# Feed-forward of a two-layer decoder trunk: down's block differences made during gate/up on VectorE and kept in DRAM, roundings moved from GpSimd to ScalarE

## The chip, the cores and the metric

The kernel runs on one core of one Trainium2 chip. The metric is device time in microseconds (us) of one execution. Engines are named as the profile names them: PE (TensorE), DVE (VectorE), ACT (ScalarE), POOL (GpSimd), SP (SyncE, whose queue issues every DMA here).

## The reference

One sequence of 1024 tokens, width 1024, passes two residual layers (an attention mixer, then a feed-forward of hidden width 2816), and a last RMSNorm. Only the feed-forward is touched:

```python
def swiglu(h, w_gate, w_up, w_down):
    return (jax.nn.silu(h @ w_gate) * (h @ w_up)) @ w_down

for layer in range(DEPTH):                  # DEPTH = 2
    ...
    h = rmsnorm(x, norm_ffn[layer])
    x = x + swiglu(h, ffn_w_gate[layer], ffn_w_up[layer], ffn_w_down[layer])
return rmsnorm(x, norm_final)
```

## The kernel before

All products are float32. Each operand is split into a rounded part `hi` (type float32r) and the rest `lo = x - hi`, and `mm3` issues three matmuls for a pair (hi·hi, hi·lo, lo·hi). `round_to` makes `hi` (a copy on ACT or a `tensor_scalar` on POOL), and `rest_of` makes `lo` with one two-operand subtraction.

The feed-forward uses Strassen-like 2x2 block products: seven instead of eight, at the price of sums and differences of blocks. `ffn` has three stages for each layer (names begin with f0 or f1):

- `ffn_prep` finishes the output projection, normalizes, and makes the blocks b11, b21, b22 and the differences t1 to t4 of the activations, all kept in SBUF as hi and lo.
- `gate_up(p)`, for p from 0 to 10, takes 256 hidden columns. For gate (g) and for up (u) it loads two 512 KB tiles `raw` (tag "raw", three buffers for the whole kernel), splits a11, a12, a22, forms s1 to s4 from them (`f0g5u` and the like are the tiles of these sums) and splits those. `product` runs seven block products of 12 matmuls each, so a p has 168 matmuls of 512 columns. PSUM results are drained into tiles ea, e4, e7; silu and the multiplication by u follow, then s1, s2, s4, s3 of the activations (ec, ed). Seven activation blocks go to DRAM (`act_da`, `act_ds`).
- `down` runs seven left blocks m (the table `plan`) against right blocks of w_down, each over four row tiles t: 28 steps (m, t) of 33 matmuls, 924 in all. A step needs its activation tile (`load_act`: two loads `ar`, rounding on ACT, rest, names f0a0 to f0a27) and the right block's hi and lo (`weights(m)`: six pieces d0 to d2, loads `dr`, names f0d00 to f0d62). After each step the result in PSUM (tile o, two buffers) is added to one to four accumulators `c`.

Before, a right block with a sign in the plan is made inside `down` from the block before it: a fresh piece of w_down is loaded, and hi and lo of the previous piece are subtracted from it by two two-operand instructions, the first always on POOL, the second on POOL or DVE in turn:

```python
    ph, pl = (v.bitcast(F32) for v in before[u // 2][1])
    second = nc.vector if u % 4 else nc.gpsimd
    if sign < 0:
        nc.gpsimd.tensor_tensor(raw, raw, ph, op=ALU.subtract)
        second.tensor_tensor(raw, raw, pl, op=ALU.subtract)
```

Each engine runs its own instructions in the program's order, and so does SP with the DMAs. That order is written by a scheduler which ranks instructions by a simulated timeline; a buffer is given to a new tile when the old one's last reader is through.

Of the kernel before, what the change touches and what calls it, by code (L numbers as in the profile page):

```python
# [11 lines left out]
F32 = mybir.dt.float32  # L12
F32R = mybir.dt.float32r
# [26 lines left out]
def trunk(ctx: ExitStack, tc: tile.TileContext, x, norm_mix, norm_ffn, norm_final,  # L40
# [89 lines left out]
    def unit8(name, b, f, hl):  # L130
        return hp.tile([128, 4, 512], F32R, name=name, tag=f"h{b}{f}{hl}")
# [698 lines left out]
    def gate_up(layer, p, name, fp, h):  # L830
        def weights(src, nm):
            raw = []
            for b in range(2):
                r = wp.tile([128, 1024], F32, name=f"{nm}r{b}", tag="raw", bufs=3).rearrange("p (k n) -> p k n", n=256)
                nc.sync.dma_start(r, src[b * 512:(b + 1) * 512, p * 256:(p + 1) * 256].rearrange("(k p) n -> p k n", p=128))
                raw.append(r)
            a11, a21, a12, a22 = (raw[b][:, :, i * 128:(i + 1) * 128] for b in range(2) for i in range(2))
            w = {}
            hl = fp.tile([128, 2, 4, 128], F32R, name=f"{nm}a", tag="wa", bufs=2)
            hl = [hl[:, i] for i in range(2)]  # L840
            early = nc.vector if p == 0 else nc.gpsimd
            round_to(nc.gpsimd if p else nc.scalar, hl[0], a11)
            rest_of(nc.vector, hl[1], a11, hl[0])
            w["a11"] = [(hl[0][:, k, :], hl[1][:, k, :]) for k in range(4)]

            def two(keys, src, wpool, tag, hi_eng, bufs):
                hi, lo = (wpool.tile([128, 1024], F32R, name=f"{nm}{keys[0]}{x}", tag=tag + t, bufs=bufs)
                          .rearrange("p (k n) -> p k n", n=256) for x, t in (("h", "hi"), ("l", "lo")))
                round_to(hi_eng, hi, src)
                rest_of(nc.vector, lo, src, hi)  # L850
                for i, key in enumerate(keys):
                    cs = slice(i * 128, (i + 1) * 128)
                    w[key] = [(hi[:, k, cs], lo[:, k, cs]) for k in range(4)]

            two(("a12", "a22"), raw[1], wp, "w", nc.gpsimd, 3)
            u1, u2 = (fp.tile([128, 4, 256], F32, name=f"{nm}u{i}", tag="wu", bufs=2) for i in range(2))
            s2, s3, s1, s4 = u1[:, :, 0:128], u1[:, :, 128:256], u2[:, :, 0:128], u2[:, :, 128:256]
            early.tensor_tensor(s1, a21, a22, op=ALU.add)
            early.tensor_tensor(s2, s1, a11, op=ALU.subtract)
            early.tensor_tensor(s3, a11, a21, op=ALU.subtract)  # L860
            two(("s2", "s3"), u1, fp, "vw", nc.scalar, 3)
            early.tensor_tensor(s4, a12, s2, op=ALU.subtract)
            two(("s1", "s4"), u2, fp, "vw", nc.scalar, 3)
            return w

        def product(src, nm):

            w = weights(src, nm)
            a, c, b = ps_s(f"{nm}oa")[:, 0, :], ps_t(f"{nm}oc"), ps_t(f"{nm}ob")
            ea = fp.tile([128, 2, 512], F32, name=f"{nm}ea", tag="ea", bufs=3)  # L870
            e = {k: fp.tile([128, 512], F32, name=f"{nm}e{k}", tag=f"e{k}", bufs=n) for k, n in ((4, 3), (7, 1))}
            e[1], e[2] = ea[:, 0], ea[:, 1]

            def times(o, left, right, start):

                for k in range(4):
                    r = tuple(v[:, k, :] for v in h[right])
                    mm3(o, w[left][k], r, start and k == 0, k == 3, not start)

            times(a, "a11", "b11", True)  # L880
            nc.scalar.copy(e[1], a)
            times(c, "a12", "b21", True)
            nc.vector.tensor_tensor(e[1], c, e[1], op=ALU.add)
            times(a, "s2", "t2", False)
            nc.scalar.copy(e[2], a)
            times(b, "s3", "t3", True)
            nc.scalar.copy(e[7], b)
            times(a, "s1", "t1", False)
            nc.scalar.copy(e[4], a)
            nc.gpsimd.tensor_tensor(e[4], e[4], e[7], op=ALU.add)  # L890
            times(b, "a22", "t4", False)
            nc.vector.tensor_tensor(e[2], b, e[2], op=ALU.add)
            times(a, "s4", "b22", False)
            return [e[1], a, e[2], e[4]]

        g = product(ffn_w_gate[layer], f"{name}g{p}")
        u = product(ffn_w_up[layer], f"{name}u{p}")
        def store(key, v):
            q = p // 6
            nc.sync.dma_start(act_d[key, q][:, :, p - q * 6, :].rearrange("t p c -> p t c"),  # L900
                              v.rearrange("p (t c) -> p t c", c=128))
# [12 lines left out]
        add.tensor_tensor(s1, av["a21"], av["a22"], op=ALU.add)
        store("s1", s1)
        add.tensor_tensor(s2, s1, av["a11"], op=ALU.subtract)
        store("s2", s2)
        add.tensor_tensor(s4, av["a12"], s2, op=ALU.subtract)
        store("s4", s4)
        add.tensor_tensor(av["a21"], av["a11"], av["a21"], op=ALU.subtract)  # L920
        store("s3", av["a21"])

    def down(layer, name, fq, fp, last):

# [6 lines left out]
        plan = (("a11", 0, 0, 0, ((0, 0), (0, 1), (1, 0), (1, 1))),
                ("s1", 0, 1, -1, ((0, 1), (1, 1))),
                ("s2", 1, 1, -1, ((0, 1), (1, 0), (1, 1))),
                ("a22", 1, 0, -1, ((1, 0),)),
                ("a12", 1, 0, 0, ((0, 0),)),
                ("s4", 1, 1, 0, ((0, 1),)),
                ("s3", 0, 1, 1, ((1, 0), (1, 1))))

        w = {}

        def weights(m):
            _, bi, bj, sign, _ = plan[m]
            before = w.get(m - 1)
            w[m] = []
            for u in range(0, nk, 2):
                if u % 4 == 0:
                    i = u // 4
                    if m % 2:
                        hl = [unit8(f"{name}d{m}{i}{x}", (0, 0, 1)[i], (0, 1, 0)[i], x) for x in "hl"]
                    else:  # L950
                        hl = [fq.tile([128, 4, 512], F32R, name=f"{name}d{m}{i}{x}", tag=f"q{('b21', 't3', 't1')[i]}{x}")
                              for x in "hl"]
                n = min(2, nk - u)
                raw = wp.tile([128, 1024], F32, name=f"{name}dr{m}{u}", tag="raw", bufs=3)[:, :n * 512]
                raw = raw.rearrange("p (k n) -> p k n", n=512)
                nc.sync.dma_start(raw, w_down[bi][:, u:u + n, bj * 512:(bj + 1) * 512])
                if sign:
                    ph, pl = (v.bitcast(F32) for v in before[u // 2][1])
                    second = nc.vector if u % 4 else nc.gpsimd
                    if sign < 0:  # L960
                        nc.gpsimd.tensor_tensor(raw, raw, ph, op=ALU.subtract)
                        second.tensor_tensor(raw, raw, pl, op=ALU.subtract)
                    else:
                        nc.gpsimd.tensor_tensor(raw, ph, raw, op=ALU.subtract)
                        second.tensor_tensor(raw, raw, pl, op=ALU.add)
                hi, lo = (v[:, u % 4:u % 4 + n, :] for v in hl)
                round_to(nc.scalar if sign or u % 4 else nc.gpsimd, hi, raw)
                rest_of(nc.vector, lo, raw, hi)
                w[m].append((u, (hi, lo)))
                yield  # L970
# [5 lines left out]
        def load_act(s):  # L976
            m, t = divmod(s, 4)
            whole = s % 2 and m < 6
            if whole:
                both = [hp.tile([128, nk, 128], F32R, name=f"{name}a{s}{x}", tag=f"h11{x}") for x in "hl"]  # L980
            out_ = []
            for g, (k0, k1) in enumerate(GROUPS):
                raw = fp.tile([128, 1024], F32, name=f"{name}ar{s}{g}", tag="wu", bufs=2)[:, :(k1 - k0) * 128]
# [258 lines left out]
```

## Time and profile before

| | before |
|---|---|
| median of 3 runs | 2891.46 us (2885.41 to 2892.29) |
| profiled execution, its own time | 2894.9 us |
| span of the profile | 2893.1 us |
| PE busy, share of the span | 2689.0 us, 93% |
| DVE, ACT, POOL busy | 1835.9, 1183.9, 1246.5 us |
| mean granted TensorE clock | 0.969 |

The span is what the profile's times are counted in, from its start at 0. Layer 0's feed-forward lies between about 780 and 1518 us in it, layer 1's between about 2160 and the end.

### The profile page before, as it was taken

The numbers are of one execution on the slowest core, as the hardware profiler recorded it, in microseconds if no ns is written. First come the engines' busy times: TensorE is split into PE (matmuls) and PEld (weight loads), VectorE is DVE, ScalarE is ACT, GpSimd is POOL, SyncE is SP. The second block draws the span as 40 slices with busy tenths as digits, with TensorE's granted clock in tenths as the row PEclk, the third lists the DMA queues.
The fourth block names the chain that finished last, engine by engine and source line by source line (L and its number), as shares of the span: only waits on it lengthen the run. The fifth ranks groups of instructions, "written<-read, shape, count | busy, mean of one in ns | idle before, by whom it ended". The sixth has DMA issues, their size and how long they took to land.

```text
span 2893.1 us, 42415 instructions
## 1 busy us (share of the span) xinstructions
PE 2689.0 (93%) x15596; PEld 2324.1 (80%) x15596; DVE 1835.9 (63%) x2822; ACT 1183.9 (41%) x2545; POOL 1246.5 (43%) x1119
## 2 busy tenths in 40 slices
PE   8999999989889999987999899999888999998798
PEld 7989898988868888866778788787886888886676
DVE  7477677565484444379654867778848444447965
ACT  4277666454252222222333555555415222222233
POOL 3566554543156656446352021212015656554623
PEclk9999999999989999999999999999998999999999
DMA  5100000113523333454553333324452333345454
GB/s 152 45 9 22 9 21 21 52 44 104 175 83 109 106 109 103 136 187 150 181 172 78 71 79 69 92 71 105 131 179 88 110 106 109 97 141 186 148 183 138
DMA packets 285855, 301.54 MB, mean 104 GB/s; under 512 B 22448, under 2 KB 233040, under 8 KB 285648
## 3 DMA queue, kind: packets, MB, share of 16 engines
q1 hardware_dynamic: 285648, 298.83, 34.5%
q8 instruction: 124, 2.03, 0.3%
q14 instruction: 83, 0.68, 0.1%
HBM read 200.72 MB, written 72.88 MB: 95 GB/s over the span
## 4 chain that ended last, share of the span: by engine, by line
PE 62%; DVE 15%; issue 8%; DMA 7%; ACT 4%; POOL 3%; SPq 0%; POOLq 0%; DVEq 0%; ACTq 0%
PE sqo L126 2%; PE sqo L127 2%; PE sqo L128 2%; DMA f0dr<-in_ffn_w_down_dram 1%; PE svo L126 1%; PE svo L127 1%; PE svo L128 1%; DMA f1ar<-act_da 1%; PE oao L126 1%; PE oao L127 1%; PE oao L128 1%; DVE f0c L1015 1%; DVE f1c L1015 1%; DMA f1dr<-in_ffn_w_down_dram 1%; DMA f0ar<-act_da 1%
## 5 line engine op out<-in xcount | busy, mean ns | idle before, releaser
L208 PEld LDWEIGHTS <-ident_b 128*128 128x128 bf16 x352 | 34.3, 97 | 47.9 <-issue 35.2
L690 POOL TENSOR_SCALAR obh<-obr 128x1024 fp32r<-128x1024 f32 (+1 forms) x8 | 12.1, 1528 | 88.1 <-DMA obr<-o2T_d 44.4
L1015 DVE TENSOR_TENSOR f1c<-f1o,f1c 128x512 f32<-128x512 f32 x56 | 36.0, 681 | 15.8 <-PE f1o L128 15.8
L1015 DVE TENSOR_TENSOR f0c<-f0o,f0c 128x512 f32<-128x512 f32 x56 | 35.9, 680 | 3.4 <-PE f0o L128 3.4
L1045 DVE TENSOR_TENSOR sv<-svo,sv 128x128 fp32r<-128x128 f32 x64 | 18.2, 286 | 29.8 <-ACT sv L1044 29.7
L1044 ACT CAST sv<-svo 128x128 fp32r<-128x128 f32 x64 | 16.9, 268 | 48.6 <-PE svo L128 36.1
L721 DVE TENSOR_TENSOR xr<-oao,xr 128x256 f32<-128x256 f32 x32 | 13.5, 423 | 22.6 <-PE oao L128 20.3
L1074 DVE TENSOR_TENSOR kc<-sqo,kc 128x512 fp32r<-128x512 f32 x16 | 11.0, 690 | 23.6 <-ACT kc L1073 23.5
L721 DVE TENSOR_TENSOR xr<-obo,xr 128x256 f32<-128x256 f32 x32 | 13.3, 419 | 19.1 <-PE obo L128 18.8
L1069 DVE SCALAR_TENSOR_TENSOR qc<-sqo,qc 128x512 fp32r<-128x512 f32 x16 | 11.0, 687 | 18.5 <-ACT qc L1068 18.5
L113 POOL TENSOR_SCALAR sqk21h<-sqk21r 128x1024 fp32r<-128x1024 f32 x1 | 1.0, 1047 | 48.2 <-PE svo L128 48.2
L1073 ACT CAST kc<-sqo 128x512 fp32r<-128x512 f32 x16 | 9.4, 587 | 30.4 <-PE sqo L128 30.2
L126 PE MATMUL cgo<-cgh,hah 128*128 128x280 f32 x64 | 19.5, 305 | 1.7 <-ACT hah L192 1.7
L113 POOL TENSOR_SCALAR sqk61h<-sqk61r 128x1024 fp32r<-128x1024 f32 x1 | 1.0, 1047 | 45.0 <-PE svo L128 45.0
L113 POOL TENSOR_SCALAR sqk41h<-sqk41r 128x1024 fp32r<-128x1024 f32 x1 | 1.0, 1047 | 44.8 <-PE svo L128 44.8
L128 PE MATMUL cgo<-cgh,hal 128*128 128x280 f32 x64 | 19.9, 311 | 0.0
L127 PE MATMUL kso<-ksl,hah 128*128 128x256 f32 x64 | 18.3, 287 | 1.2 <-POOL ksl L115 1.2
L126 PE MATMUL q1o<-q1h,hah 128*128 128x256 f32 x64 | 19.4, 303 | 0.0
L127 PE MATMUL cgo<-cgl,hah 128*128 128x280 f32 x64 | 19.4, 303 | 0.0
L126 PE MATMUL kso<-ksh,hah 128*128 128x256 f32 x64 | 18.2, 288 | 0.9 <-ACT gates L395 0.9
L128 PE MATMUL q1o<-q1h,hal 128*128 128x256 f32 x64 | 18.9, 295 | 0.0
L126 PE MATMUL dk3o<-dk3h,hah 128*128 128x256 f32 x64 | 18.7, 293 | 0.0
(10123 smaller groups left out, 11762.3 us busy)
## 6 DMA issues: line engine op xcount, KB each, us to landing
f0dr<-in_ffn_w_down_dram SPq DMA_DIRECT2D x35, 512.0 KB, 4.6
f1dr<-in_ffn_w_down_dram SPq DMA_DIRECT2D x35, 512.0 KB, 4.6
x_d<-xr SPq DMA_DIRECT2D x64, 128.0 KB, 2.3
ks<-kc SPq DMA_DIRECT2D x64, 128.0 KB, 2.3
f0ar<-act_ds SPq DMA_DIRECT2D x16, 384.0 KB, 3.5
f1ar<-act_ds SPq DMA_DIRECT2D x16, 384.0 KB, 3.0
act_ds<-f0ec SPq DMA_DIRECT2D x22, 256.0 KB, 2.3
act_ds<-f0ed SPq DMA_DIRECT2D x22, 256.0 KB, 2.3
```

The source lines that it names most:

```text
L126: nc.tensor.matmul(o, a[0], b[0], start=start, stop=False, skip_group_check=onto)
L127: nc.tensor.matmul(o, a[0], b[1], start=False, stop=False, skip_group_check=onto)
L128: nc.tensor.matmul(o, a[1], b[0], start=False, stop=stop, skip_group_check=onto)
L208: nc.tensor.matmul(s[:, b, mo:mo + 128], ident_b, m, start=False, stop=i == len(here) - 1)
L690: nc.gpsimd.tensor_scalar(hs, raw, 1.0, 1.0, op0=ALU.mult, op1=ALU.mult)
L721: nc.vector.tensor_tensor(xr, o[:, :256], xr, op=ALU.add)
L1015: nc.vector.tensor_tensor(cv, o, cv, op=ALU.add)
L1044: nc.scalar.copy(vs[j][:, tt, :, 0:64], src)
L1045: nc.vector.tensor_tensor(vs[j][:, tt, :, 64:128], src, vs[j][:, tt, :, 0:64].bitcast(F32), op=ALU.subtract)
L1069: nc.vector.scalar_tensor_tensor(lo, o, SCALE, hi.bitcast(F32), op0=ALU.mult, op1=ALU.subtract)
L1073: nc.scalar.copy(kc[:, 0, :], o)
L1074: nc.vector.tensor_tensor(kc[:, 1, :], o, kc[:, 0, :].bitcast(F32), op=ALU.subtract)
```

## The change

The four block differences that `down` needs as right factors are made once, in `gate_up(p)`: two tiles t of 128x1024 for each p (tag "raw" too) are filled with the four blocks of w_down of that p by two DMAs each, DVE makes four differences in place, and one DMA writes the tile to a DRAM buffer `t_d`. In `down`, `weights(m)` loads either a plain block of w_down or the ready difference from `t_d`, so the two subtractions for each piece are gone. In gate/up the sums s1 to s4 of weights and of activations go from POOL to DVE; the drain of e4 becomes one DVE addition straight from PSUM in place of an ACT copy and a POOL addition. Roundings that POOL did go to ACT. The activation tiles of odd steps and three right blocks exchange their places in SBUF (h11 and h00, and so on). Nothing outside the feed-forward is edited.

```diff
+    t_d = [dp.tile([4, 128, HT // 2, 512], F32, name=f"t_d{i}") for i in range(2)]
...
-            early = nc.vector if p == 0 else nc.gpsimd
-            round_to(nc.gpsimd if p else nc.scalar, hl[0], a11)
+            round_to(nc.scalar, hl[0], a11)
...
-            two(("a12", "a22"), raw[1], wp, "w", nc.gpsimd, 3)
+            two(("a12", "a22"), raw[1], wp, "w", nc.scalar, 3)
...
-            early.tensor_tensor(s1, a21, a22, op=ALU.add)
-            early.tensor_tensor(s2, s1, a11, op=ALU.subtract)
-            early.tensor_tensor(s3, a11, a21, op=ALU.subtract)
+            nc.vector.tensor_tensor(s1, a21, a22, op=ALU.add)
+            nc.vector.tensor_tensor(s2, s1, a11, op=ALU.subtract)
+            nc.vector.tensor_tensor(s3, a11, a21, op=ALU.subtract)
...
             times(a, "s1", "t1", False)
-            nc.scalar.copy(e[4], a)
-            nc.gpsimd.tensor_tensor(e[4], e[4], e[7], op=ALU.add)
+            nc.vector.tensor_tensor(e[4], a, e[7], op=ALU.add)
...
-        add.tensor_tensor(s1, av["a21"], av["a22"], op=ALU.add)
+        nc.vector.tensor_tensor(s1, av["a21"], av["a22"], op=ALU.add)
...
+        for c in range(2):
+            r = wp.tile([128, 1024], F32, name=f"{name}t{p}{c}", tag="raw", bufs=3).rearrange("p (j n) -> p j n", n=256)
+            for i in range(2):
+                rows = slice((2 * p + i) * 128, (2 * p + i + 1) * 128)
+                nc.sync.dma_start(r[:, 2 * i:2 * i + 2, :], ffn_w_down[layer][rows, :]
+                                  .rearrange("k (j n) -> k j n", j=2)[:, :, c * 256:(c + 1) * 256])
+            b11, b12, b21, b22 = (r[:, i, :] for i in range(4))
+            nc.vector.tensor_tensor(b11, b12, b11, op=ALU.subtract)
+            nc.vector.tensor_tensor(b12, b22, b12, op=ALU.subtract)
+            nc.vector.tensor_tensor(b22, b22, b11, op=ALU.subtract)
+            nc.vector.tensor_tensor(b21, b21, b22, op=ALU.subtract)
+            nc.sync.dma_start(t_d[layer][:, :, p, c * 256:(c + 1) * 256].rearrange("t k n -> k t n"), r)
...
-                        hl = [unit8(f"{name}d{m}{i}{x}", (0, 0, 1)[i], (0, 1, 0)[i], x) for x in "hl"]
+                        hl = [unit8(f"{name}d{m}{i}{x}", (1, 1, 0)[i], (1, 0, 1)[i], x) for x in "hl"]
...
-                nc.sync.dma_start(raw, w_down[bi][:, u:u + n, bj * 512:(bj + 1) * 512])
-                if sign:
-                    ph, pl = (v.bitcast(F32) for v in before[u // 2][1])
-                    second = nc.vector if u % 4 else nc.gpsimd
-                    if sign < 0:
-                        nc.gpsimd.tensor_tensor(raw, raw, ph, op=ALU.subtract)
-                        second.tensor_tensor(raw, raw, pl, op=ALU.subtract)
-                    else:
-                        nc.gpsimd.tensor_tensor(raw, ph, raw, op=ALU.subtract)
-                        second.tensor_tensor(raw, raw, pl, op=ALU.add)
+                if isinstance(right, tuple):
+                    bi, bj = right
+                    nc.sync.dma_start(raw, w_down[bi][:, u:u + n, bj * 512:(bj + 1) * 512])
+                else:
+                    nc.sync.dma_start(raw, t_d[layer][right, :, u:u + n, :])
                 hi, lo = (v[:, u % 4:u % 4 + n, :] for v in hl)
-                round_to(nc.scalar if sign or u % 4 else nc.gpsimd, hi, raw)
+                round_to(nc.scalar, hi, raw)
...
-                both = [hp.tile([128, nk, 128], F32R, name=f"{name}a{s}{x}", tag=f"h11{x}") for x in "hl"]
+                both = [hp.tile([128, nk, 128], F32R, name=f"{name}a{s}{x}", tag=f"h00{x}") for x in "hl"]
...
-                rest_of(nc.gpsimd if m == 6 else nc.vector, lo, raw, hi)
+                rest_of(nc.vector, lo, raw, hi)
```

The scheduler writes other orders for it. The first place is DVE in the middle of layer 0's gate/up, around the drain of e4 of gate 6. Before, these rows stood there (f0g7a12l and the like are rests of the weights, f0g6ea drains PSUM):

```order
L769 TENSOR_TENSOR f0u6s1l<-f0u6u_13923,f0u6s1h 128x1024
L769 TENSOR_TENSOR f0u7a<-f0u7r_14176,f0u7a 128x512
L892 TENSOR_TENSOR f0g6ea<-f0g6ob,f0g6ea 128x512
L769 TENSOR_TENSOR f0u7a12l<-f0u7r_14178,f0u7a12h 128x1024
L883 TENSOR_TENSOR f0u6ea<-f0u6oc,f0u6ea 128x512
```

and now these:

```order
L770 TENSOR_TENSOR f0u6s1l<-f0u6u_14008,f0u6s1h 128x1024
L859 TENSOR_TENSOR f0g7u_14165<-f0g7u_14166,f0g7r_14154 128x4x128
L860 TENSOR_TENSOR f0g7u_14165<-f0g7r_14154 128x4x128
L862 TENSOR_TENSOR f0g7u_14166<-f0g7r_14156,f0g7u_14165 128x4x128
L770 TENSOR_TENSOR f0u7a<-f0u7r_14275,f0u7a 128x512
L889 TENSOR_TENSOR f0g6e_13904<-f0g6oa,f0g6e_13905 128x512
L927 TENSOR_TENSOR f0t_14417<-f0t_14417 128x256
L928 TENSOR_TENSOR f0t_14417<-f0t_14417 128x256
L929 TENSOR_TENSOR f0t_14417<-f0t_14417 128x256
L891 TENSOR_TENSOR f0g6ea<-f0g6ob,f0g6ea 128x512
L930 TENSOR_TENSOR f0t_14417<-f0t_14417 128x256
L770 TENSOR_TENSOR f0u7a12l<-f0u7r_14277,f0u7a12h 128x1024
```

Between the same neighbours DVE now also has three sums of the next weights (L859 to L862), the drain of e4 from PSUM (L889) and the four differences of one t tile (L927 to L930).

The second place is SP in the same stretch. Before, the load of f0u6r was followed by f0g7r, the store act_da of f0g5ea and the other f0g7r. The rows now:

```order
L836 DMA f0u6r_13998<-in_ffn_w_up_dram 128x4x256
L924 DMA f0t_14138<-in_ffn_w_down_dram 128x2x256 x2
L931 DMA t_d_102<-f0t_14138 128x4x256
L899 DMA act_da_104<-f0g5ea 128x4x128
L924 DMA f0t_14146<-in_ffn_w_down_dram 128x2x256 x2
L931 DMA t_d_102<-f0t_14146 128x4x256
L836 DMA f0g7r_14154<-in_ffn_w_gate_dram 128x4x256
```

The second t tile's load stands behind a store of activations (act_da), and both loads of the next gate weights (f0g7r) behind the second write of t_d.

The third place is DVE where down of layer 0 begins. Before:

```order
L909 TENSOR_TENSOR f0ec_15093<-f0ec_15093,f0u10oa 128x512
L962 TENSOR_TENSOR f0dr_15218<-f0dr_15218,f0d00l 128x1024
L914 TENSOR_TENSOR f0ec_15093<-f0ec_15093,f0g10e_14878 128x512
L769 TENSOR_TENSOR f0a1l<-f0ar_15198,f0a1h 128x768
L769 TENSOR_TENSOR f0a1l<-f0ar_15202,f0a1h 128x640
```

and now:

```order
L770 TENSOR_TENSOR f0a1l<-f0ar_15354,f0a1h 128x768
L770 TENSOR_TENSOR f0d02l<-f0dr_15308,f0d02h 128x512
L891 TENSOR_TENSOR f0u10ea<-f0u10ob,f0u10ea 128x512
L770 TENSOR_TENSOR f0a1l<-f0ar_15358,f0a1h 128x640
L907 TENSOR_TENSOR f0g10ea<-f0g10ea,f0u10ea 128x512
L907 TENSOR_TENSOR f0ec_15233<-f0ec_15233,f0u10oa 128x512
```

The rest of step 1's activations (f0a1l) stood behind a difference of the next right block (L962) and behind the product of gate/up's last PSUM bank (f0u10oa); now it stands ahead of that product, and there is no difference.

## Rows read from the trace of the kernel before

**Rows 1.** Page, busy us of an engine, share of the span, instructions.

```profile
PE 2689.0 (93%) x15596; PEld 2324.1 (80%) x15596; DVE 1835.9 (63%) x2822; ACT 1183.9 (41%) x2545; POOL 1246.5 (43%) x1119
```

**Rows 2.** Windows: stretch, length, PE, PEld, DVE, ACT, POOL busy; clock, DMA share, GB/s.

```profile
836.00:1240.00 404.00, 403.83 (x1782) 334.07 (x1781) 183.78 (x177) 120.78 (x176) 228.94 (x183) 1.00 0.38 111
1240.00:1507.00 267.00, 229.93 (x965) 185.02 (x964) 200.78 (x179) 82.02 (x108) 135.49 (x63) 0.94 0.56 181
2211.00:2616.00 405.00, 404.50 (x1783) 334.72 (x1784) 184.39 (x177) 120.78 (x176) 229.16 (x183) 1.00 0.37 110
2616.00:2880.00 264.00, 230.29 (x956) 184.98 (x955) 202.41 (x177) 80.33 (x104) 126.69 (x60) 0.94 0.54 173
1389.40:1434.20 44.80, 44.80 (x199) 37.13 (x198) 27.11 (x27) 12.39 (x16) 15.33 (x8) 1.00 0.61 198
```

**Rows 3.** Waits of PE between 1259 and 1380 us: total, times, longest.

```profile
PE f0o L126 <- DVE f0c L1015: 12.1, 4, 4.5
PE f0o L128 <- DVE f0a1l L769: 10.6, 1, 10.6
PE f0o L128 <- DVE f0a9l L769: 3.8, 1, 3.8
```

**Rows 4.** Timeline of PE: start, us, line, out<-in.

```profile
828.23 0.77 PE L126 MATMUL f0g0oc<-f0b21h,f0g0a12h 128*128 128x512 f32 x1
...
836.00 0.40 PE L126 MATMUL f0g0oa<-f0b11h,f0g0a 128*128 128x512 f32 x1
...
1396.85 0.39 PE L126 MATMUL f0o<-f0d30h,f0a140hi 128*128 128x512 f32 x1
...
1434.25 0.39 PE L126 MATMUL f0o<-f0d40h,f0a19h 128*128 128x512 f32 x1
...
1479.41 0.39 PE L126 MATMUL f0o<-f0d60h,f0a240hi 128*128 128x512 f32 x1
...
1516.67 0.39 PE L128 MATMUL f0o<-f0d62h,f0a271lo 128*128 128x512 f32 x1
...
2203.55 0.76 PE L126 MATMUL f1g0oc<-f1b21h,f1g0a12h 128*128 128x512 f32 x1
...
2884.28 0.39 PE L128 MATMUL f1o<-f1d62h,f1a271lo 128*128 128x512 f32 x1
```

**Rows 5.** Timeline of DVE where down begins; idle before, releaser in brackets.

```profile
1260.99 3.34 DVE L962 TENSOR_TENSOR f0dr<-f0dr,f0d00l 128x1024 f32<-128x1024 f32 x1 [4.54 <-POOL f0dr L961]
1264.26 2.84 DVE L914 TENSOR_TENSOR f0ec<-f0ec,f0g10e 128x512 f32<-128x512 f32 x1
1267.02 3.82 DVE L769 TENSOR_TENSOR f0a1l<-f0ar,f0a1h 128x768 fp32r<-128x768 f32 x2
1270.77 0.68 DVE L916 TENSOR_TENSOR f0ed<-f0ec,f0g10ea 128x512 f32<-128x512 f32 x1
...
1271.97 1.21 DVE L769 TENSOR_TENSOR f0d10l<-f0dr,f0d10h 128x1024 fp32r<-128x1024 f32 x1
```

**Rows 6.** Timeline of POOL in the same stretch.

```profile
1260.91 2.34 POOL L962 TENSOR_TENSOR f0dr<-f0dr,f0d00l 128x1024 f32<-128x1024 f32 x1
1263.21 3.34 POOL L961 TENSOR_TENSOR f0dr<-f0dr,f0d01h 128x1024 f32<-128x1024 f32 x1
```

**Rows 7.** Groups by line: busy us, mean ns of one; idle before, releaser.

```profile
L721 DVE TENSOR_TENSOR xr<-oao,xr 128x256 f32<-128x256 f32 x32 | 13.5, 423 | 22.6 <-PE oao L128 20.3 <-DMA x_d<-xr 1.7
L764 ACT CAST f0d11h<-f0dr 128x1024 fp32r<-128x1024 f32 x2 | 2.1, 1048 | 0.0
```

**Rows 8.** DMA issues, the first between 1386 and 1436 us alone: count, KB, us to landing.

```profile
f0dr<-in_ffn_w_down_dram SPq DMA_DIRECT2D x8, 512.0 KB, 5.4
...
f0g5r<-in_ffn_w_gate_dram SPq DMA_DIRECT2D x2, 512.0 KB, 4.3
f0x<-x_d SPq DMA_DIRECT2D x8, 512.0 KB, 7.5
xm_d<-f0x SPq DMA_DIRECT2D x8, 512.0 KB, 3.3
```

More of the change, by code (lines that the diff above doesn't have):

```diff
@@ L853, in two @@
                     w[key] = [(hi[:, k, cs], lo[:, k, cs]) for k in range(4)]
-            two(("a12", "a22"), raw[1], wp, "w", nc.gpsimd, 3)
+            two(("a12", "a22"), raw[1], wp, "w", nc.scalar, 3)
             u1, u2 = (fp.tile([128, 4, 256], F32, name=f"{nm}u{i}", tag="wu", bufs=2) for i in range(2))
             s2, s3, s1, s4 = u1[:, :, 0:128], u1[:, :, 128:256], u2[:, :, 0:128], u2[:, :, 128:256]
-            early.tensor_tensor(s1, a21, a22, op=ALU.add)
-            early.tensor_tensor(s2, s1, a11, op=ALU.subtract)
-            early.tensor_tensor(s3, a11, a21, op=ALU.subtract)
+            nc.vector.tensor_tensor(s1, a21, a22, op=ALU.add)
+            nc.vector.tensor_tensor(s2, s1, a11, op=ALU.subtract)
+            nc.vector.tensor_tensor(s3, a11, a21, op=ALU.subtract)
             two(("s2", "s3"), u1, fp, "vw", nc.scalar, 3)
-            early.tensor_tensor(s4, a12, s2, op=ALU.subtract)
+            nc.vector.tensor_tensor(s4, a12, s2, op=ALU.subtract)
             two(("s1", "s4"), u2, fp, "vw", nc.scalar, 3)
@@ L913, in gate_up @@
         s1, s2, s4 = ec[:, 1], ed[:, 0], ed[:, 1]
-        add.tensor_tensor(s1, av["a21"], av["a22"], op=ALU.add)
+        nc.vector.tensor_tensor(s1, av["a21"], av["a22"], op=ALU.add)
         store("s1", s1)
-        add.tensor_tensor(s2, s1, av["a11"], op=ALU.subtract)
+        nc.vector.tensor_tensor(s2, s1, av["a11"], op=ALU.subtract)
         store("s2", s2)
-        add.tensor_tensor(s4, av["a12"], s2, op=ALU.subtract)
+        nc.vector.tensor_tensor(s4, av["a12"], s2, op=ALU.subtract)
         store("s4", s4)
-        add.tensor_tensor(av["a21"], av["a11"], av["a21"], op=ALU.subtract)
+        nc.vector.tensor_tensor(av["a21"], av["a11"], av["a21"], op=ALU.subtract)
         store("s3", av["a21"])
+        for c in range(2):
[10 more added lines that the diff above has]
+            nc.sync.dma_start(t_d[layer][:, :, p, c * 256:(c + 1) * 256].rearrange("t k n -> k t n"), r)
     def down(layer, name, fq, fp, last):
@@ L929, in down @@
         c = {}
[L931 to L937, printed above, removed]
+        plan = (("a11", (0, 0), ((0, 0), (0, 1), (1, 0), (1, 1))),
+                ("s1", 0, ((0, 1), (1, 1))),
+                ("s2", 3, ((0, 1), (1, 0), (1, 1))),
+                ("a22", 2, ((1, 0),)),
+                ("a12", (1, 0), ((0, 0),)),
+                ("s4", (1, 1), ((0, 1),)),
+                ("s3", 1, ((1, 0), (1, 1))))
         w = {}
         def weights(m):
-            _, bi, bj, sign, _ = plan[m]
-            before = w.get(m - 1)
+            right = plan[m][1]
             w[m] = []
@@ L999, in down @@
         home = {0: (wp, "whi"), 1: (wp, "wlo"), 2: (wp, "whi"), 3: (fp, "ec"), 7: (fp, "ed")}
-        for m, (_, _, _, _, into) in enumerate(plan):
+        for m, (_, _, into) in enumerate(plan):
             prep = weights(m + 1) if m < 6 else iter(())
```

1 line of the change is left out of this document (removed).

## Prediction

> **What bounds the kernel now.** The page gives PE 93% of the span, with DVE at 63% and POOL at 43% [rows 1], so the question is where PE's missing 7% lies and how fast PE can go at all. I read the windows by stage next. In gate/up of both layers PE is busy 403.83 of 404 us and 404.50 of 405 us; in down it is busy 229.93 of 267 and 230.29 of 264 us, at a mean clock of 0.94, while DVE, at 200.78 of 267 us, has its heaviest stretch [rows 2]. So gate/up has nothing to give, and down has.
>
> PE's best pace comes from the timeline: step (3, 2) of down starts at 1396.85 and step (4, 3) at 1434.25 [rows 4], five steps of 33 matmuls later, so one matmul takes 37.40 / 165 = 0.2267 us. The window around it has PE busy all of 44.80 us at clock 1.00 [rows 2]. A layer has 11 x 168 + 924 = 2772 of these matmuls, 628.4 us at that pace. Layer 0 takes 1516.67 + 0.23 - 828.23 = 688.7 us and layer 1 takes 2884.28 + 0.23 - 2203.55 = 681.0 us [rows 4], so they lose 60.3 and 52.6 us.
>
> Some of that stays whatever is done here. The 18th matmul of layer 0 starts at 836.00, 7.8 us after the first, where 17 x 0.2267 = 3.9 would do [rows 4]: 3.9 us for the start, taken for both layers. Layer 0's last block starts at 1479.41 and so takes 37.5 us to its end [rows 4] where 132 matmuls need 29.9: 7.6 us for the next layer's transposes and norms. What is left is 48.8 us in layer 0 and 48.7 us in layer 1, **97.5 us**, and it lies in down's blocks 0 to 5.
>
> The waits of PE say what ends them: between 1259 and 1380 us PE waited 12.1 us for additions from PSUM on DVE, 10.6 us for the rest of step 1's activations, 3.8 us for another such rest [rows 3]. All are DVE, in its queue. The timeline says why DVE is late. A 128x1024 subtraction takes 1.21 us at 1271.97, but 3.34 us at 1260.99 and a 128x512 addition takes 2.84 us at 1264.26, where the next one takes 0.68 us [rows 5]; at those moments POOL runs two-operand instructions of 2.34 and 3.34 us [rows 6]. The 4.54 us before the first of them is a wait for POOL's half of the difference [rows 5]. So down loses its time to the differences twice: as links of the chain on POOL, and because they stretch DVE's own work.
>
> **What the change takes away.** For each layer 24 of 42 pieces of right blocks lose two subtractions, all of POOL's and the 12 of DVE, and every other two-operand POOL instruction of gate/up and down goes too. What is then left in down on DVE: for a block, rests of the right block (5 x 1.21 + 0.69 = 6.7 us), rests of activations (eight of 768 or 640 columns, estimated at 0.96 or less from 1.21 for 1024 and 0.68 for 512 [rows 5]: 7.7 us) and additions (16, 8 or 12 in blocks 0 to 2, 4 in the others but the last, at 0.68). Block 0 is the heaviest with 6.7 + 7.7 + 10.9 = 25.3 of the 29.9 us that PE needs; the others have 23 or less. ACT has some 12 us. The trace has a model of that state: blocks 3 and 4 before, whose next right blocks have no sign, ran 1389.40 to 1434.20 without a gap at 198 GB/s [rows 2]. Later blocks need the same bytes, from t_d in place of w_down, in runs twice as long.
>
> At the head of down the new order has the first half of f0a1l ahead of the drain of u10's last bank. The inputs of that rest come from DMAs and ACT copies that run under PE's work on gate/up's last product and step 0; by my reading of the order both halves are there some 5 us before PE reaches step 1. The 10.6 us go, and the stretch at the lower clock after them. What stays is bunching in block 0, where eight additions, four rests and the next block's rests meet. Bounds: nothing, as in blocks 3 and 4, and 15 us a layer, about half of the waits [rows 3] with the matmuls at the lower clock that follow. I take 5 us a layer, near the model's end, since block 0 has 4.6 us of room. So down gives back 97.5 - 10 = **87.5 us**, or 67.5 to 97.5 by the bounds.
>
> **What gate/up has to carry.** DVE's work for one p, now: six 128x1024 rests at 1.21 (7.3 us), 24 instructions of 128x512 at 0.68 (16.3 us: 2 rests, 8 weight sums, 6 drains, 4 products, 4 activation sums) and eight of 128x256. The trace has none of those with both operands in SBUF; the nearest, with one operand in PSUM, takes 0.42 [rows 7], so 3.4 us. Sum 27.0 of the 168 x 0.2267 = 38.1 us that PE needs. The bounds of the 0.42 are half a 512 (0.34) and a whole one (0.68): 26.3 to 29.0. ACT: six 1024 copies at 1.05 [rows 7], nine or so of 128x512 at about 0.6 and four silus, some 14 us. Neither is the bound.
>
> The Trainium skill (Perfetto Trace Analysis, Optimizing Scalar/DVE Operations) advises the other direction: if DVE is saturated, give work to ScalarE or even GpSimd, though it adds that GpSimd shares a read port with DVE. By the rows its condition is not met, 27.0 of 38.1 us; were it met, each us over 38.1 would cost 22 us in the two layers' 22 p.
>
> What can stop PE there is order. DVE now waits in its queue for t tiles, and SP has a serial chain: write t, load the other t, write it, load the next gate weights. The place from which it hurts is the product of u's last PSUM bank: DVE reaches it behind the rest of the next gate's a12, and PE needs that bank again 27 matmuls (6.1 us) into the next p, at 44.2 us after the p began; minus 1.21 + 2 x 0.68 for the instructions there, the rest must start by 41.6 us. The chain: SP's act_da store ahead of the second t load waits for a drain 75 matmuls in and a product, 17.0 + 1.4 = 18.4 us; load 4.3 [rows 8], four differences and three instructions among them 4, write 3.3, next weights 4.3, rounding 1.1: 35.4 us, and with SP's issue and queueing about 1 us more, 36.4. There are **5 us of slack a p**. The drain of e4, new on DVE, has 23 matmuls (5.2 us) between its bank's last write and the next; it had 22 for ACT's copy. So gate/up costs nothing under PE's cover; if the cover goes, each us beyond the slack costs 20 us (ten p in two layers).
>
> **The sum.** 2894.9 - 87.5 = 2807.4 us against the profiled execution's own time. That lies 3.4 us above the median of 2891.46, so the prediction for a median is 2891.5 - 87.5 = **2804 us**.
>
> **Rivals.**
> - *Block 0 to 2 keep half their waits.* For it: DVE's queue is fixed by a simulated order, and one late DMA holds all behind it; 12.1 us of the waits are additions queued in DVE [rows 3]. Against: those additions sit behind instructions that took two to three times their length. Gain 97.5 / 2, about 49 us: 2843 us.
> - *The chain of t tiles holds gate/up: slower than before.* Each p moves about 2 MB more than the 111 GB/s of now [rows 2], some 55 GB/s. If loads come to the 7.5 us that eight in a row took [rows 8] and the write grows as much (to 5.8), the chain is 2 x 3.2 + 2.5 = 8.9 us longer, 3.9 beyond the slack, 78 us lost: 2882 us. It decides from 4.4 us beyond the slack (87.5 / 20); at 7 us beyond it the time is 2891.5 - 87.5 + 140 = 2944 us. Against: at 198 GB/s, more than gate/up would then move, loads took 5.4 us [rows 8]; that is 2 x 1.1 us more, inside the slack.
> - *The stretched DVE instructions have another cause than POOL,* the DMA traffic or the memory. Then only the removed links gain, POOL's part of the chain, and DVE goes on late with more to do: about no gain, 2890 us. Against: 1.21 us and 3.34 us stand within 11 us of each other of one another, under the same traffic [rows 5], and only POOL differs [rows 6].
>
> **Chances.** Forecast (2789 to 2822) 0.64; half the waits stay (2822 to 2865) 0.21; chain or cause eat most of the gain (2865 to 2885) 0.06; no change 0.03; slower 0.06. Change and no change part at 0.3%, 9 us, which is what these runs can tell (they spread over 7 us). Faster 0.91, same 0.03, slower 0.06. For 8 in 10 the range is 2788 to 2848: the forecast's own 2789 to 2822, and the upper side out to a half-kept down.
>
> **What would show it.** Right: gate/up's windows still full; DVE there near 27 us a p; no DVE subtraction of 128x1024 above 1.3 us in gate/up or down; steps of down 7.48 us apart but for a few in block 0; PE's waits in down under 10 us a layer; clock near 1.00. Wrong: PE waiting in gate/up for L889 or for weights behind L927 to L930; 3 us instructions on DVE with POOL idle; steps of 9 to 12 us in blocks 1 and 2; loads in gate/up landing after 6 us or more.

## The result, and the profile after

| | before | after |
|---|---|---|
| median | 2891.88 us of 4 runs (2885.41 to 2895.16) | 2807.84 us of 4 runs (2806.78 to 2817.6) |
| ratio, 95% interval | | 0.972 (0.9692 to 0.9747) |
| profiled execution, span | 2894.9, 2893.1 us | 2817.6, 2815.8 us |

The kernel became 84 us faster; 2804 us were forecast. The profiled execution of after is the slowest of its four, 9 us above the next, so the losses read from it are at the upper end. The page and its chain of waits [rows 1]:

```profile
PE 2668.3 (95%) x15596; PEld 2314.0 (82%) x15596; DVE 1886.3 (67%) x3274; ACT 1246.2 (44%) x2603; POOL 538.5 (19%) x645
...
PE 76%; DVE 11%; DMA 5%; ACT 3%; issue 3%; POOL 1%; SPq 0%; DVEq 0%; ACTq 0%; POOLq 0%
```

The windows (stretch, length, busy us of PE, PEld, DVE, ACT, POOL; clock, DMA share, GB/s): gate/up and down of layer 0, then of layer 1 [rows 2], then p = 0, 1 and 2 of layer 0.

```profile
836.00:1240.00 404.00, 398.68 (x1748) 328.94 (x1749) 269.90 (x403) 138.99 (x192) 0.00 (x0) 1.00 0.54 167
1240.00:1470.00 230.00, 229.32 (x1028) 189.30 (x1027) 146.58 (x185) 96.37 (x125) 14.12 (x13) 1.00 0.65 215
2170.00:2580.00 410.00, 406.06 (x1783) 335.04 (x1782) 271.67 (x406) 142.34 (x197) 0.00 (x0) 1.00 0.54 165
2580.00:2806.00 226.00, 222.99 (x972) 184.07 (x971) 140.11 (x174) 88.33 (x112) 3.84 (x7) 0.98 0.62 204
829.00:867.00 38.00, 35.93 (x148) 28.93 (x148) 28.57 (x44) 19.01 (x26) 0.43 (x1) 0.94 0.48 145
867.00:905.00 38.00, 33.63 (x141) 27.00 (x140) 27.43 (x43) 12.38 (x19) 0.00 (x0) 0.96 0.54 166
905.00:943.00 38.00, 38.00 (x169) 31.48 (x168) 26.04 (x40) 13.24 (x19) 0.00 (x0) 1.00 0.54 166
```

PE in down went from 230 of 267 us to 229 of 230: nearly no gap is left. Gate/up, full before, has gaps now, but only in the first values of p, two in layer 0 and three in layer 1; in layer 0 PE is busy 38.00 of 38 us a p from 905 on. Of the three windows by p the first lost time before the change too (36.39 us busy), the second hardly (37.83). The timeline of PE gives the two stages their lengths: the first product of gate/up, the first of down, the last of down in layer 0.

```profile
828.97 0.80 PE L126 MATMUL f0g0oc<-f0b21h,f0g0a12h 128*128 128x512 f32 x1
...
1251.06 0.39 PE L126 MATMUL f0o<-f0d00h,f0a00hi 128*128 128x512 f32 x1
...
1474.49 0.39 PE L128 MATMUL f0o<-f0d62h,f0a271lo 128*128 128x512 f32 x1
```

Gate/up takes 1251.06 - 828.97 = 422.1 us, down 1474.49 + 0.23 - 1251.06 = 223.7 us. In the profile of before down of layer 0 began here:

```profile
1243.35 0.39 PE L126 MATMUL f0o<-f0d00h,f0a00hi 128*128 128x512 f32 x1
```

So by [rows 4] the two took 415.1 and 273.6 us. In every kernel here the last 36 matmuls of gate/up come after down's first, among its first step, so that step takes 15.64 us where nothing waits. The table has the two lengths for every kernel, from its profiled execution; each interval is against runs of before made beside it, whose medians lay between 2891.0 and 2893.6 us. The experiments are told below.

| kernel | median, us | ratio to before, 95% | gate/up, layer 0, 1 | down, layer 0, 1 |
|---|---|---|---|---|
| before | 2891.88 | | 415.1, 415.5 | 273.6, 265.5 |
| after | 2807.84 | 0.9692 to 0.9747 | 422.1, 421.0 | 223.7, 223.7 |
| e1, sums of gate/up on POOL | 2879.24 | 0.994 to 0.9973 | 454.8, 456.8 | 224.1, 219.4 |
| e2, idle POOL work, two operands | 2844.92 | 0.9822 to 0.988 | 420.0, 420.7 | 243.7, 236.3 |
| e3, idle POOL work, one operand | 2815.6 | 0.9716 to 0.9757 | 418.6, 416.3 | 229.1, 224.0 |
| e4, differences in down, on DVE | 2817.3 | 0.9714 to 0.9758 | 414.8, 416.2 | 236.1, 228.1 |
| e6, tiles made later | 2816.0 | 0.972 to 0.9749 | 423.6, 423.4 | 225.3, 221.0 |
| e7, tiles' DMAs in POOL's queue | 2812.38 | 0.9705 to 0.9735 | 421.9, 422.6 | 226.6, 221.6 |
| e8, sums on POOL, no tiles | 2797.2 | 0.9654 to 0.9683 | 414.7, 416.3 | 223.5, 217.6 |
| e9, no subtractions in p = 0 to 2 | 2806.69 | 0.9683 to 0.9719 | 418.7, 417.6 | 224.1, 219.8 |
| e10, tiles' subtractions on POOL | 2849.82 | 0.9836 to 0.9879 | 442.3, 441.5 | 223.7, 218.9 |
| e11, all of the tiles' work on POOL | 2810.02 | 0.969 to 0.9739 | 420.6, 420.2 | 224.9, 219.2 |
| e12, gate/up's half of the change alone | 2874.46 | 0.9924 to 0.9957 | 416.4, 414.7 | 265.8, 258.1 |
| e13, as e11, tiles made later | 2842.71 | 0.9822 to 0.985 | 438.5, 431.7 | 224.0, 218.9 |

Of DVE's groups (mean ns after the bar; idle before, releaser) between 905 and 1240 us these answer to [rows 5] and to the 0.42 of [rows 7]; the first subtraction of a tile carries the waits for its loads:

```profile
L927 DVE TENSOR_TENSOR f0t<-f0t 128x256 f32<-128x256 f32 x17 | 7.2, 425 | 30.8 <-DMA f0t<-in_ffn_w_down_dram 30.8
...
L770 DVE TENSOR_TENSOR f0g5a12l<-f0g5r,f0g5a12h 128x1024 fp32r<-128x1024 f32 x1 | 1.2, 1226 | 2.4 <-ACT f0g5a12h L765 2.4
```

PE's waits from 836 to 1250 us (total, times, longest) name where gate/up lost (the 1.6 us for f0g0a stood there before the change too), and the timelines of DVE, ACT and SP why:

```profile
PE f0u1oa L126 <- DVE f0ec L907: 3.7, 1, 3.7
PE f0g0oa L128 <- DVE f0g0a L770: 1.6, 1, 1.6
PE f0u0oa L126 <- DVE f0u0e L889: 0.7, 1, 0.7
```

```profile
877.69 0.43 DVE L927 TENSOR_TENSOR f0t<-f0t 128x256 f32<-128x256 f32 x1 [1.79 <-DMA f0t<-in_ffn_w_down_dram]
...
883.86 0.69 DVE L770 TENSOR_TENSOR f0g2a<-f0g2r,f0g2a 128x512 fp32r<-128x512 f32 x1 [2.63 <-ACT f0g2a L765]
885.70 1.23 DVE L770 TENSOR_TENSOR f0g2a12l<-f0g2r,f0g2a12h 128x1024 fp32r<-128x1024 f32 x1 [1.15 <-ACT f0g2a12h L765]
886.85 0.68 DVE L907 TENSOR_TENSOR f0ec<-f0ec,f0u0oa 128x512 f32<-128x512 f32 x1
```

```profile
883.21 0.62 ACT L765 CAST f0g2a<-f0g2r 128x512 fp32r<-128x512 f32 x1 [8.52 <-DMA f0g2r<-in_ffn_w_gate_dram]
...
874.58 1.20 SPq L924 DMA_DIRECT2D f0t<-in_ffn_w_down_dram  x2
875.94 1.03 SPq L836 DMA_DIRECT2D f0g2r<-in_ffn_w_gate_dram  x2
```

The product at 886.85 frees the PSUM bank that PE wants for u1. It stands in DVE's queue behind two rests of g2's weights, and these wait for weights that came late: SP issued their loads behind a tile's load. When PE went on after its 3.7 us, its first matmuls took 0.63 us for the usual 0.39, and the window 867 to 905 has a mean clock of 0.96. In layer 1 the waits are 2.1 us at g2 (for a drain on ACT), 1.3 at u1 and 0.6 at g1.

### The profile page after: what moved, and what is told of

It reads as the page before. It is cut to its first block, busy times and chain, and to the rows that moved or that the text cites. A ratio compares the mean times of both kernels' runs of the same rounds, so it can differ in the third digit from the quotient of the medians.

```text
span 2815.8 us, 42506 instructions
## 1 busy us (share of the span) xinstructions
PE 2668.3 (95%) x15596; PEld 2314.0 (82%) x15596; DVE 1886.3 (67%) x3274; ACT 1246.2 (44%) x2603; POOL 538.5 (19%) x645
## 4 chain that ended last, share of the span: by engine, by line
PE 76%; DVE 11%; DMA 5%; ACT 3%; issue 3%; POOL 1%; SPq 0%; DVEq 0%; ACTq 0%; POOLq 0%
PE f1o L126 2%; PE f1o L128 2%; PE f1o L127 2%; PE f0o L128 2%; PE f0o L126 2%; PE f0o L127 2%; PE sqo L126 2%; PE sqo L127 2%; PE sqo L128 2%; PE svo L126 1%; PE svo L128 1%; PE svo L127 1%; PE oao L126 1%; PE oao L127 1%; PE oao L128 1%
## 5 line engine op out<-in xcount | busy, mean ns | idle before, releaser
L927 DVE TENSOR_TENSOR f0t<-f0t 128x256 f32<-128x256 f32 x22 | 9.4, 425 | 39.0 <-DMA f0t<-in_ffn_w_down_dram 39.0
L927 DVE TENSOR_TENSOR f1t<-f1t 128x256 f32<-128x256 f32 x22 | 9.4, 426 | 35.8 <-DMA f1t<-in_ffn_w_down_dram 35.8
L128 PE MATMUL cgo<-cgh,hal 128*128 128x280 f32 x64 | 20.1, 313 | 0.0
```

The costliest lines, as they stand in the source:

```text
L128: nc.tensor.matmul(o, a[1], b[0], start=False, stop=stop, skip_group_check=onto)
L927: nc.vector.tensor_tensor(b11, b12, b11, op=ALU.subtract)
```

## Experiments

The question was how much of the 92 us in down came from POOL's presence and what from the links of the chain, and why gate/up, costed at nothing, lost 12.5 us in the profiled execution.

**e4: the links without POOL.** In down the differences as before, all on DVE; no tiles; gate/up's sums on DVE as in after. Against before, in part:

```diff
-                    second = nc.vector if u % 4 else nc.gpsimd
+                    second = nc.vector
...
-                        nc.gpsimd.tensor_tensor(raw, raw, ph, op=ALU.subtract)
+                        nc.vector.tensor_tensor(raw, raw, ph, op=ALU.subtract)
...
```

> The differences are made in down again, from the halves of the block before as in the kernel before, but with every subtraction on DVE and none on POOL; gate/up makes no differences and keeps its sums on DVE. It has the links of the chain without POOL beside them. If the links as such were the loss, most of the 91.7 us comes back: about 2870 us. If POOL's presence was, DVE has in blocks 1, 2, 3 and 6 some 6 units x 3 x 1.21 us plus 11 us of other work, about 31 us for 29.9 us of matmuls, a loss of 0 to 3 us a block or up to 24 us in all, and gate/up gets back its 12.5 us: 2795 to 2820 us.

2817.3 us, inside the range given for POOL's presence: the links as such were not most of the loss. Window 1281 to 1311 in down's blocks 0 and 1:

```profile
1281.00:1311.00 30.00, 29.05 (x126) 23.09 (x125) 29.37 (x36) 10.79 (x13) 0.00 (x0) 1.00 0.62 209
```

DVE is busy 29.37 of 30 us and still keeps PE at 29.05. Down is 12.4 and 4.4 us a layer longer than after, gate/up 7.3 and 4.8 us shorter, and the interval overlaps that of the change.

**e2 and e3: POOL without the links.** Useless work on POOL in down's blocks 1, 2, 3 and 6, with two SBUF operands or one:

```diff
+                for k in list(range(n)) * ((2 if u % 4 == 0 else 1) if m in (1, 2, 3, 6) else 0):
+                    nc.gpsimd.tensor_tensor(idle, hi[:, k, :].bitcast(F32), hi[:, k, :].bitcast(F32), op=ALU.subtract)
                 rest_of(nc.vector, lo, raw, hi)
```

> The changed kernel with useless work added: in down, on the rounded halves of blocks 1, 2, 3 and 6, POOL subtracts two 128x512 operands in SBUF into a scratch tile that nobody reads, about as much a block (17 instructions, some 22 to 28 us) as before the change. No link of the chain to the matmuls is added. If POOL's two-operand work stretches DVE's, as the prediction has it, DVE's 128x1024 subtractions beside it go from 1.21 us to 2.3 to 3.4 us, DVE is near 30 of 30 us in these blocks, and part of the 91.7 us comes back: 2820 to 2860 us. If the stretched DVE came from the DMA traffic or from the links, the subtractions stay at 1.2 to 1.3 us and the kernel at 2808 us (2802 to 2814).

> The same useless work with one SBUF operand instead of two (a scaling by 1), as many instructions on the same tiles at the same places. If it is the second operand that stretches DVE, the subtractions stay near 1.21 us and the kernel at 2808 us (2802 to 2815); if any work of POOL does, it comes out as the two-operand form does, 2820 to 2860 us.

Groups of DVE between 1251 and 1341 us, the first with two operands (e2), the second with one (e3):

```profile
L770 DVE TENSOR_TENSOR f0d11l<-f0dr,f0d11h 128x1024 fp32r<-128x1024 f32 x2 | 4.1, 2055 | 0.0
```

```profile
L770 DVE TENSOR_TENSOR f0d11l<-f0dr,f0d11h 128x1024 fp32r<-128x1024 f32 x2 | 3.3, 1628 | 0.0
```

With two operands DVE's subtraction went from 1.22 to 2.06 us (short of the 2.3 expected), and 37 us came back, with nothing added to the chain. With one operand it still went to 1.43 to 1.63 us, against what I expected; the time, 2815.6 us, is just outside the expected bound and not to be told from after's. The useless work also reads the rounded halves and so keeps their buffers longer; e3 reads the same, but in less time (POOL busy 84 us for 118 in layer 0's down), so it rules that out only in part. The waits of PE in e2, from 1244 to 1400 us, name DVE, as before the change [rows 3], for additions and rests of activations:

```profile
PE f0o L126 <- DVE f0c L1022: 6.6, 2, 4.8
PE f0o L128 <- DVE f0a40lo L770: 3.2, 1, 3.2
```

**e12 and e1: the two halves of the change apart.** e12 is before with gate/up's sums and roundings off POOL; e1 is after with them back on POOL:

```diff
+            early = nc.vector if p == 0 else nc.gpsimd
...
-            nc.vector.tensor_tensor(s1, a21, a22, op=ALU.add)
+            early.tensor_tensor(s1, a21, a22, op=ALU.add)
...
```

> The kernel before with the other half of the change alone: gate/up's sums and roundings off POOL as changed, no difference tiles, down as before with its differences on POOL and DVE. If the gain lies in down alone, as the prediction has it, gate/up stays at about 415.3 us a layer, down at about 273 and 265 us, and the kernel at 2891 us (2882 to 2900). If taking POOL's work out of gate/up gave part of the gain (through down's start, whose first tiles come out of the last p), it is 2885 us or less.

> The changed kernel with the sums and the two roundings of gate/up back on POOL; down and the making of the differences stay as changed. Down should keep its 223.7 us a layer whatever the theory, since nothing in it changes. Gate/up lost 6.9 and 5.6 us a layer in its first three p. Theory A (the loads of the differences stand in SP's queue ahead of the next weights): they stand there still, gate/up stays at about 421 us a layer, the kernel at 2808 us (2802 to 2814). Theory B (the sums that DVE took over hold its queue): gate/up goes back to about 415.3 us, the kernel to 2796 us. With POOL's two-operand work beside it the 128x1024 subtractions on DVE in gate/up should stretch from 1.21 us to the 1.8 to 2.3 us that they took before.

e12 gave 2874.5 us, its second case: gate/up unchanged, down 7.8 and 7.4 us a layer shorter. So 17 of the 84 us come with taking POOL's sums away. The head of down gains nothing by itself: step (0, 1) of layer 0 took 11.0 us for 21.1 before, but the other three of block 0 grew by 11.2 together. The gain stands in block 1, whose first matmul and block 2's are, in before and then in e12:

```profile
1296.69 0.39 PE L126 MATMUL f0o<-f0d10h,f0a40hi 128*128 128x512 f32 x1
...
1340.61 0.51 PE L126 MATMUL f0o<-f0d20h,f0a80hi 128*128 128x512 f32 x1 [4.50 <-DVE f0c L1015]
```

```profile
1299.32 0.39 PE L126 MATMUL f0o<-f0d10h,f0a40hi 128*128 128x512 f32 x1
...
1334.83 0.39 PE L126 MATMUL f0o<-f0d20h,f0a80hi 128*128 128x512 f32 x1
```

That is 43.9 and 35.5 us, in layer 1 43.9 and 37.1. Down's own instructions are the same in both, but the scheduler's order is not, and no run shows which difference in it counts.

e1 gave 2879.2 us, and neither theory had it: with the sums on POOL beside the tiles gate/up loses some 40 us a layer against before. Its waits from 829 to 1300 us, of PE (two of nine such) and of DVE:

```profile
PE f0u4oa L126 <- DVE f0ec L910: 5.3, 1, 5.3
PE f0u7oa L126 <- DVE f0ec L910: 2.9, 1, 2.9
```

```profile
DVE f0t L930 <- DMA f0t<-in_ffn_w_down_dram: 59.3, 20, 5.6
...
DVE f0u8a L770 <- POOL f0u8a L767: 8.0, 1, 8.0
```

DVE is busy only half of the time there, but its queue stands 8.0 us a p for POOL and 3.0 us on average for a tile's load, and the product that frees u's last bank stands behind both, in nearly every p.

**e8: e1 without the tiles,** down loading stored blocks in their place.

> The kernel with gate/up's sums and two roundings on POOL, as in the first experiment, but without the difference tiles: gate/up makes none, and down loads blocks of the stored weight in their place, so its weights are not the reference's. The first experiment lost about 34 us a layer in gate/up against the changed kernel, 40 against the kernel before. If the loss comes only of both together (DVE's queue, which stands up to 8 us at a time behind POOL, and the tiles' subtractions and buffers in it), gate/up is back at 415.5 us a layer and the kernel at about 2795 us. If POOL's sums alone cost it, with the new order around them, gate/up stays at 440 to 455 us and the kernel above 2850 us.

2797.2 us, gate/up full. Window 836 to 1240:

```profile
836.00:1240.00 404.00, 404.00 (x1784) 334.51 (x1783) 184.60 (x177) 121.59 (x178) 228.28 (x182) 1.00 0.37 111
```

So e1's loss is of both together. e8 also gives a price for the tiles in the changed kernel: 2807.8 - 2797.2 = 10.6 us. (The two also differ in where the sums are made; but e4, with the sums on DVE and no tiles, has gate/up as short, 414.8 and 416.2 us.)

**e6, e7, e9: what of the tiles costs that.** Made later (e6), loads and writes in POOL's queue (e7), without the subtractions of the first three p (e9), in this order:

```diff
+        for q in ((), (), (), (0, 1), (2, 3), (4, 5), (6, 7), (8,), (9,), (10,), ())[p]:
...
-                nc.sync.dma_start(r[:, 2 * i:2 * i + 2, :], ffn_w_down[layer][rows, :]
+                nc.gpsimd.dma_start(r[:, 2 * i:2 * i + 2, :], ffn_w_down[layer][rows, :]
...
+            if p > 2:
```

> The changed kernel with the difference tiles made later: none in p = 0 to 2, two p's worth in each of p = 3 to 6, one in p = 7 to 9, none in p = 10. If gate/up lost its 6.9 and 5.6 us because the tiles take buffers, queue places and DVE time while the weights have no lead yet, the loss goes: gate/up about 415.5 us a layer, the kernel at 2795 us (2790 to 2801). If the tiles cost this wherever they stand, or p = 3 to 6 with double work has too little room (38.0 us a p, DVE busy 25.6 of them now, with 3.4 us more about 29), the loss stays or grows: 2808 us or more.

> The changed kernel with the loads and the write of the difference tiles issued by POOL's queue, which has nothing else in gate/up, in place of SP's. Buffers and DVE's work are unchanged. If the place in SP's queue ahead of the weights is what costs gate/up its 12.5 us, the kernel goes to 2796 us. If it is the buffers that the tiles share with the weights, or the DVE work, it stays at 2808 us (2803 to 2813).

> The changed kernel without the four subtractions of the difference tiles of p = 0 to 2: the tiles are loaded and written as before, with the weights themselves in the place of the differences, so part of the weights of down is not the reference's. It takes 24 subtractions, about 10 us of DVE a layer, out of the first three p and leaves loads, writes and buffers. If DVE's time there is the cause, gate/up goes to 415.5 us a layer and the kernel to 2796 us; if loads, queue places or buffers are, it stays at 2808 us (2803 to 2813).

None recovers the time. e7, at 2812.4 us within its second range, shows that the place in SP's queue alone is not the cause, and e6, at 2816.0, that the early place of the tiles alone is not. In e6 the first three p have no such wait, and p = 4 to 6 wait instead (f0g5oa 2.4 us, f0g6oa 1.5 us, for ACT's drain). In e7 the loss is spread over g2 to g5 (2.4, 0.7, 0.5, 0.9 us). e9 is inconclusive: gate/up is 3.4 us a layer shorter than in after's profiled execution, but that was the slowest of its four, and the median is only 1.2 us lower, within the spread.

**e10, e11, e13: the tiles' subtractions on POOL** (e10), their DMAs in POOL's queue too (e11), and that with no half tile in p = 0 and 1, three a p in p = 2 to 5 (e13).

```diff
-            nc.vector.tensor_tensor(b11, b12, b11, op=ALU.subtract)
+            nc.gpsimd.tensor_tensor(b11, b12, b11, op=ALU.subtract)
...
```

> The changed kernel with the eight 128x256 subtractions of the difference tiles of each p on POOL in place of DVE; loads and writes stay in SP's queue. DVE's queue then never stands at a tile that has not landed, and has 3.4 us a p less. Theory A (the tiles cost gate/up because their subtractions stand in DVE's queue ahead of the drain that PE waits for): gate/up goes back to about 416 us a layer and the kernel to 2796 us (2790 to 2801). Theory B (any two-operand work of POOL in gate/up stretches DVE enough to hold PE, as in the first experiment): eight instructions of about 0.6 us, a quarter of 2.34 us each, stretch DVE by up to 5 us a p, PE waits a p, gate/up 425 us or more and the kernel above 2812 us.

> As the run with the subtractions on POOL, and the tiles' loads and writes issued by POOL's queue too, so that neither SP's nor DVE's queue holds any of this work; only the buffers are still shared. Theory A: 2796 us or a little less (2789 to 2800), since a late tile holds nothing but POOL. If the shared buffers are the cause, gate/up stays at 421 us a layer in this run and in the one before, and the kernel at 2808 us.

> As the run with all of the tiles' work on POOL and its queue, where gate/up waited only in p = 0 and 1 (38.00 of 38.00 us from p = 2 on) and took 420.5 us a layer; here no half tile is made in p = 0 and 1, three in each of p = 2 to 5, two in each of p = 6 to 10. If the loss is that the tiles take buffers and time while the weights have no lead, gate/up goes to 415.5 us a layer and the kernel to 2797 us (2790 to 2801). If it moves with the tiles to p = 2 to 5, as in the run that made them later on DVE, gate/up stays at 420 us or more and the kernel at 2808 us or more.

e10 is 42 us slower than after, e11 is not to be told from after: the two do the same work, and only the queue of the tiles' DMAs differs. Waits of SP's queue from 905 to 1240 us in e10:

```profile
SPq L931 <- POOL f0t L930: 65.4, 17, 4.3
...
SPq L836 <- DMA t_d<-f0t: 21.5, 8, 4.0
```

SP's write waits for POOL's last difference, and the next gate weights stand behind it; each p PE then waits 1.2 to 3.3 us, for a drain on ACT. So e10's range for theory B held, but not by B's cause: with the DMAs off that queue (e11) the same subtractions on POOL leave PE at 38.00 of 38 us from p = 2 on. e13 went the second way, but much further than its bounds of 420 and 2808 us suggest: gate/up 438.5 and 431.7 us, the kernel 2842.7 us, with waits of 7.2, 2.7 and 6.2 us in p = 3 to 5. Its SP queue, 905 to 1290 us:

```profile
SPq L836 <- DMA t_d<-f0t: 68.9, 12, 10.8
```

A weight load (L836) waits up to 10.8 us for a tile's write, although these are in different queues there: what they share is the three "raw" buffers. In after the same wait is 33.4 us in 11 times between 836 and 1240 us. By itself it costs nothing: in e11 it is 50.3 us in 8 times from 905 to 1240 us, and PE is full there. That the buffers are the cause of the remaining 10.6 us fits e6, e7, e11 and e13, but tiles with buffers of their own weren't tried, so it stays argued. The tiles' traffic is a rival that no run sets apart: the loads of g2's weights took this long to land (us, the last number) in after, then in e8, which has no tiles:

```profile
f0g2r<-in_ffn_w_gate_dram SPq DMA_DIRECT2D x2, 512.0 KB, 7.6
```

```profile
f0g2r<-in_ffn_w_gate_dram SPq DMA_DIRECT2D x2, 512.0 KB, 4.5
```

They were also issued later in after, by 19 us for the first of the two and 7 us for the second, and that is more than the 3 us of landing.

## Why the prediction was right

- **The sum.** 84.0 us by the medians, 87.5 forecast. That it is so close is in part luck: down gave 4 us more than forecast, and gate/up, put at nothing, cost some 11 to 12. (The sum's own bounds, 67.5 and 97.5 us, come to 2794 and 2824 us; the range of 2789 to 2822 is a little off them.) From before, step by step: gate/up's sums off POOL 2891.9 - 2874.5 = 17.4 (e12); POOL out of down, links kept on DVE, 2874.5 - 2817.3 = 57.2 (e4); the links gone, 2817.3 - 2797.2 = 20.1 (e8, whose sums on POOL cost gate/up nothing without tiles); the tiles' price, 10.6 us back (with the sums on DVE again). These steps come to the whole by construction and are no test of it; with each run against the runs of before beside it they are 19.1, 56.7, 18.0 and 9.8 us.
- **Down.** Forecast 87.5, found 49.9 + 41.8 = 91.7 in the profiled execution. Steps are 7.48 us apart but for a few: in layer 1 two of block 0 took 10.65 and 10.4 us, a wait of 3.0 us for additions and the slower clock behind it (0.86 granted from 2598 to 2622), 6.1 us against the 5 taken. Layer 0 has 1.4 us there, and its last block kept 4.6 us of the 7.6 that I had set aside as staying whatever is done.
- **Why down was late.** "Links of the chain on POOL, and because they stretch DVE's own work": the second is shown by e2, and it is the larger: e4 keeps the links and loses 17 us in down against after, e2 keeps POOL and loses 33, before, with both, lost 92. That the two together cost more than their sum I put down to DVE being full in before, in this window:

```profile
1304.00:1334.00 30.00, 24.66 (x95) 19.13 (x94) 30.00 (x20) 7.27 (x9) 21.36 (x9) 0.89 0.49 151
```

No run takes that apart, and e2's POOL instructions were half as wide as those of before and stretched DVE less, so the 33 us is no full measure of POOL's part. The rival of another cause than POOL falls: no 128x1024 subtraction in gate/up or down of after is above 1.3 us, at more DMA traffic.
- **Half the waits stay** did not happen: PE waits 0.7 us in down of layer 0, 3.0 in layer 1.
- **Gate/up at nothing** is the term that was mis-sized: it cost 12.5 us in the profiled execution, 10.6 by the medians with e8. DVE's load was right, 25.5 us a p for 27.0 worked out, 0.42 for the 128x256 form. What I had worked out was a p in steady state, and there it held; in the first p the weights have no lead yet. There gate/up's windows were not full, against a sign that I had named for being right, and two of the signs for being wrong showed: PE waited 0.7 us for L889 and 3.7 us for a product behind late weights, and the loads of g2's weights landed after 7.6 us.
- **The chain of tiles** did hold the place I named, the product of u's last PSUM bank, and it decides how much of the gain is left as soon as something adds to it: POOL's sums left in place add 71 us (e1), a write that waits for POOL in SP's queue 42 us (e10). I had costed the sums' move as work that DVE could bear and at no gain. It is the condition without which the tiles bring 13 us, not 84.

## What to carry to other kernels

When two engines slow each other, take the one out before redesigning the algorithm: moving down's subtractions to DVE, with gate/up's sums off POOL, came as near as these runs can tell to making the differences once and storing them. A busy share under 70% says little of an engine whose queue stands for others: price new work by what stands behind it in the queue and in shared buffers, and price the first rounds of a loop, where prefetch has no lead, apart from the steady ones.

## What the hardware showed that I had not expected

POOL with one SBUF operand also stretches DVE, 1.22 to 1.63 us for 128x1024 (e3), where two operands gave 2.06 (e2) and up to 3.4 in before. The additions of down, with one operand in PSUM, keep 0.68 us beside POOL's work in before, e2 and e3 alike. The Trainium skill (SBUF — State Buffer, Who interferes with whom) has this rule: a DVE instruction with two SBUF inputs contends with a GpSimd instruction that reads SBUF, and one with at most one SBUF input and outside the two-port modes does not. The traces agree in which instructions slow each other. The rule calls the shared ports an exclusive lock, but only for the two-port modes does it say that the loser waits for the whole of the other instruction. Here, outside those modes, the wait grew with the width of POOL's instruction: in before 128x1024 on POOL beside a 1.21 us subtraction made up to 3.4 us, in e2 half that width made 2.06, that is 2.2 us and 0.85 us more.
